# One subtraction per weight stream, moved from VectorE to GpSimd

## The chip, the cores and the metric

The kernel runs on one core of a Trainium2 chip. The metric is the device time of one execution in microseconds, here the median of three runs. The engines are named as in the profile: PE (TensorE), DVE (VectorE), ACT (ScalarE), POOL (GpSimd) and SP (the queue that issues most DMAs).

## The reference, cut to what matters

One decoder layer on 1024 tokens of width 1024. First an input projection feeds retention heads and stick-breaking attention heads, and an output projection follows; then comes a layer of experts (PEER): each token scores 2 x 128 keys in each of 8 heads, keeps 16 experts a head, and sums what these 128 experts give.

```python
proj = h @ w_in                                        # 1024 x 3584
mixed = concatenate([y_ret, y_sb], -1) @ w_out         # 1024 x 1024
x = x + gate1 * mixed
qry = (h2 @ w_query).reshape(T, 8, 2, 128)             # 1024 x 2048
top_s, top_i = top_k(einsum('thpc,hpkc->thpk', qry, sub_keys), 16)
...                                                    # best 16 of the 256 pairs, softmax gates
u = expert_down[ids];  a = einsum('pd,ped->pe', x, u)
v = expert_up[ids];    y = einsum('pe,ped->pd', gelu(a) * gates, v)
```

## The kernel before, in words

The tokens are eight tiles of 128. They go through the layer in three segments: tile 0, tiles 1 to 3, and tiles 4 to 7 (`SEGS`). A segment runs nine streams of projection weights (retention K, Q, V and gate; stick-breaking K, Q, V; two halves of the output projection) and four streams of expert query weights. A stream is 512 columns wide and walks over eight blocks of 128 rows (`kt`, 0 to 7).

In the segments of tiles 1 to 3 and 4 to 7 the matmuls are made in three passes for precision. A weight block `raw` is split into a high part `whi`, which ACT rounds (line 272), and a low part `wlo`, which is `raw - whi` (line 273). Before, the low part of block 0 is made on DVE and those of blocks 1 to 7 on POOL. PE then multiplies high by high, high by low and low by high (lines 277 to 279 or 281 to 283). `whi` and `wlo` have three buffers each, `raw` has two that hold two blocks each. There are 26 such streams, so 208 subtractions, 26 on DVE and 182 on POOL. Tile 0 uses unsplit weights.

The experts are handled in two ways. For tiles 0 to 3 POOL fetches every chosen expert's row by an indirect DMA (line 780, 256 a tile, 1024 in all: 128 of `down`, then 128 of `up`), and DVE multiplies it with the token and sums (line 791, `down`) or adds it, scaled, to the result (line 801, `up`). Each such fetch and its DVE instruction is called a gather here. There are five buffers `g`, so POOL can be at most five gathers ahead of DVE. The other operand of the DVE instruction lies in PSUM. Gathers have no place of their own in the program: they stand at its end, and the scheduler of the framework fills them in among the instructions of the segments and of the dense stage. One edge is written by hand: gathers 480 to 495 may be issued only after a certain POOL instruction of the dense stage (`HOLD`), so the first 480 lie in the segments.

Tiles 4 to 7 go through the dense stage: all 16384 experts are multiplied with the tokens on PE (lines 839 to 841 and 948 to 950). It begins when the last segment has its queries, the 16 best keys of each head (lines 674 to 678, on DVE) and the routing of tile 4 (`topk`).

All instructions of an engine run in the order that the scheduler wrote; an instruction that waits holds up what stands behind it on its engine. The scheduler decides by its own reckoning of durations, so moving one subtraction to another engine also moves its neighbours.

Of the kernel before, what the change touches and what calls it, by code (L numbers as in the profile page):

```python
# [10 lines left out]
F32 = mybir.dt.float32  # L11
# [43 lines left out]
def tile_kernel(ctx, tc, A, out):  # L55
    nc = tc.nc
    ACT, DVE, POOL, PE, SP = nc.scalar, nc.vector, nc.gpsimd, nc.tensor, nc.sync
# [12 lines left out]
    def copy(out_, in_, scale=1.0):  # L70
        ACT.activation(out_, in_, AF.Copy, scale=scale)  # L71

    def pstile(tag, bufs, shape=(128, 512)):
        return ps.tile(list(shape), F32, name=tag, tag=tag, bufs=bufs)
# [155 lines left out]
    def seg_gen(phase, t0, nt, hooks):  # L230
# [5 lines left out]
        def U(shape, dt=F32):  # L236
            return up.tile(shape, dt, name="u", tag="u")
# [10 lines left out]
        def stream(src, c0, lhs, evac, transposed):  # L248

            acc = [pstile("acc", 4) for _ in range(4 if transposed else nt)]  # L250
            for kt in range(KT):
                st, sp = kt == 0, kt == KT - 1
                if whole:
                    if kt % 2 == 0:
                        raw2 = U([128, 2, 512])
                        SP.dma_start(raw2, src[c0 // 512, kt // 2])
                    raw = raw2[:, kt % 2]
                    for i in range(len(acc)):
                        sl = slice(128 * i, 128 * i + 128)
                        if transposed:  # L260
                            PE.matmul(acc[i][:, :n], raw[:, sl], lhs[:, kt], start=st, stop=sp)
                        else:
                            PE.matmul(acc[i], lhs[:, kt, sl], raw, start=st, stop=sp)
                    continue
                if kt % 2 == 0:
                    raw2 = wp.tile([128, 2, 512], F32, name="wraw", bufs=2)
                    SP.dma_start(raw2, src[c0 // 512, kt // 2])
                raw = raw2[:, kt % 2]
                lhs_hi, lhs_lo = lhs
                hi = wp.tile([128, 512], F32R, name="whi", bufs=3)  # L270
                lo = wp.tile([128, 512], F32R, name="wlo", bufs=3)
                copy(hi, raw)
                (POOL if kt else DVE).tensor_sub(lo, raw, hi.bitcast(F32))  # L273
                for i in range(len(acc)):
                    sl = slice(128 * i, 128 * i + 128)
                    if transposed:
                        PE.matmul(acc[i][:, :n], hi[:, sl], lhs_hi[:, kt], start=st, stop=False)
                        PE.matmul(acc[i][:, :n], hi[:, sl], lhs_lo[:, kt], start=False, stop=False)
                        PE.matmul(acc[i][:, :n], lo[:, sl], lhs_hi[:, kt], start=False, stop=sp)
                    else:  # L280
                        PE.matmul(acc[i], lhs_hi[:, kt, sl], hi, start=st, stop=False)
                        PE.matmul(acc[i], lhs_hi[:, kt, sl], lo, start=False, stop=False)  # L282
                        PE.matmul(acc[i], lhs_lo[:, kt, sl], hi, start=False, stop=sp)  # L283
            for i in range(len(acc)):
                evac(i, acc[i])
            if hooks:
                hooks.pop(0)()
# [71 lines left out]
        def ev_rk(i, acc):  # L359
# [3 lines left out]
            POOL.tensor_tensor(hv(rkz[i]), hv(k), zeta[:, :, None].to_broadcast([128, 8, 64]), op=OP.mult)  # L363

        stream(A["w_in"], 512, hT_, ev_rk, False)
        if 0 < t0 < NG:
            mod_pass(5 * D, 2, lambda k: U([128, D]), V)
# [3 lines left out]
        def ev_rq(i, acc):  # L371
            q = V()
            rot(acc, q, t0 + i)
            copy(rqT[i], transpose4(q, ident))

        stream(A["w_in"], 0, hT_, ev_rq, False)
        def ev_rv(i, acc):
            copy(rv[i], acc)

        stream(A["w_in"], 1024, hT_, ev_rv, False)  # L380
        rc = [U([128, 2, 512]) for i in range((nt + 1) // 2)]
        rg = [rc[i // 2][:, i % 2] for i in range(nt)]
# [677 lines left out]
```

## Time and profile before

| | |
|---|---|
| median of 3 runs | 3123.57 us (3121.55 to 3126.93) |
| profiled execution, own time | 3128.33 us |
| its span, first to last instruction | 3126.6 us |
| segment of tile 0 | about 0 to 230 us |
| segment of tiles 1 to 3 | about 230 to 730 us |
| segment of tiles 4 to 7 | about 730 to 1440 us |
| dense stage, with the rest of the gathers | 1440 us to the end |

The profile is one execution with every instruction's start and duration. It is read by stretches: an engine that is busy all of a stretch sets its length; an engine with idle time there waits for something, and the rows say for what.

### The profile page before, as it was taken

To read this page: it belongs to the slowest core of one execution; us is meant where nothing else is said; L and a number is where in the kernel's file an instruction comes from. 1 tells how busy PE (TensorE), PEld (TensorE's weight loads), DVE (VectorE), ACT (ScalarE), POOL (GpSimd) and SP (SyncE) were. 2 spreads that over 40 slices of the span, in tenths; PEclk is the share of its full clock that TensorE was granted. 3 is DMA by queue.
4 is the path that set the end of the run, shared out by engine and by line. 5 is a ranking of instruction groups with operands and counts; after the bars stand their busy time and mean duration, and the time that the engine had idled before them with its cause. 6 is when DMAs were issued, how large, how long until landed. Compare 5 with 4: busy or idle time off the path is not lost. (4 is left out here: it accounts for less than half of the span.)

```text
span 3126.6 us, 38159 instructions
## 1 busy us (share of the span) xinstructions
PE 2688.8 (86%) x12308; PEld 2090.4 (67%) x12308; DVE 2508.4 (80%) x4619; ACT 1289.4 (41%) x2249; POOL 1913.3 (61%) x1590
## 2 busy tenths in 40 slices
PE   6967878788987687796889999899889999999996
PEld 2454654576766345584678877677768788888884
DVE  2269879899988998899899767787886777778778
ACT  1222334344333463433767634343444444444441
POOL 1025876777787766743478656556556666766664
PEclk9978985888987687897989999899999999999998
DMA  8787877998787878851389979798788998899997
GB/s 320 251 309 274 304 241 255 332 359 296 246 279 242 286 219 274 318 213 41 138 314 335 339 287 323 265 326 286 274 319 311 337 353 335 330 346 331 352 334 263
DMA packets 299882, 903.36 MB, mean 289 GB/s; under 512 B 34841, under 2 KB 102425, under 8 KB 279201
## 3 DMA queue, kind: packets, MB, share of 16 engines
q0 software_dynamic: 147456, 536.94, 48.5%
q1 hardware_dynamic: 152224, 363.98, 32.3%
q8 instruction: 97, 1.59, 0.2%
q14 instruction: 105, 0.85, 0.1%
HBM read 848.34 MB, written 52.45 MB: 288 GB/s over the span
## 5 line engine op out<-in xcount | busy, mean ns | idle before, releaser
L780 POOL DMA_INDIRECT g<-in_down_dram,ids x512 | 550.0, 1074 | 420.9 <-DVE g L791 253.7
L780 POOL DMA_INDIRECT g<-in_up_dram,ids x512 | 564.3, 1102 | 396.4 <-DVE gy L801 236.6
L801 DVE SCALAR_TENSOR_TENSOR gy<-g,a,gy 128x1024 f32<-128x1024 f32 x508 | 651.1, 1282 | 92.8 <-DMA g<-in_up_dram,ids 87.5
L791 DVE SCALAR_TENSOR_TENSOR g<-g,gy 128x1024 f32<-128x1024 f32 x512 | 612.8, 1213 | 108.7 <-DMA g<-in_down_dram,ids 107.0
L839 PE MATMUL tp<-Thi,dhi 128*128 128x512 f32 x1024 | 404.5, 395 | 26.3 <-ACT dhi L71 21.7
L948 PE MATMUL acc<-u,p 128*128 128x512 f32 x1024 | 402.7, 402 | 27.7 <-ACT acc L71 16.7
L950 PE MATMUL acc<-u,p 128*128 128x512 f32 x1024 | 389.2, 398 | 30.3 <-DVE p L925 30.3
L949 PE MATMUL acc<-u,p 128*128 128x512 f32 x1024 | 407.1, 400 | 2.9 <-POOL u L826 2.9
L840 PE MATMUL tp<-Tlo,dhi 128*128 128x512 f32 x1024 | 402.6, 393 | 0.0
L841 PE MATMUL tp<-Thi,dlo 128*128 128x512 f32 x1024 | 401.3, 393 | 0.3 <-POOL dlo L826 0.3
L826 POOL TENSOR_TENSOR u<-raw,u 128x1024 fp32r<-128x1024 f32 x128 | 309.3, 2430 | 29.9 <-ACT u L71 28.4
L273 POOL TENSOR_TENSOR wlo<-wraw,whi 128x512 fp32r<-128x512 f32 x182 | 233.9, 1296 | 74.6 <-ACT whi L71 58.4
L826 DVE TENSOR_TENSOR dlo<-raw,dhi 128x1024 fp32r<-128x1024 f32 x122 | 187.6, 1539 | 93.4 <-ACT dhi L71 92.5
L71 ACT ACTIVATE whi<-wraw 128x512 fp32r<-128x512 f32 x208 | 128.6, 629 | 322.3 <-PE acc L283 110.4
L948 PEld LDWEIGHTS acc<-u,p 128*128 128x128 f32 x1024 | 198.6, 194 | 74.8 <-ACT acc L71 19.2
L950 PEld LDWEIGHTS acc<-u,p 128*128 128x128 f32 x1024 | 196.2, 192 | 77.3 <-DVE p L925 36.3
L839 PEld LDWEIGHTS tp<-Thi,dhi 128*128 128x128 f32 x1024 | 194.2, 190 | 68.2 <-ACT dhi L71 23.6
L282 PE MATMUL acc<-wlo,Thi 128*128 128x512 f32 x504 | 213.0, 423 | 26.1 <-POOL wlo L273 24.3
L949 PEld LDWEIGHTS acc<-u,p 128*128 128x128 f32 x1024 | 199.0, 194 | 45.2 <-POOL u L826 3.3
L71 ACT ACTIVATE yacc<-acc 128x512 f32<-128x512 f32 x186 | 109.1, 594 | 283.5 <-PE acc L950 281.7
L841 PEld LDWEIGHTS tp<-Thi,dlo 128*128 128x128 f32 x1024 | 193.6, 189 | 40.9 <-POOL dlo L826 1.4
L840 PEld LDWEIGHTS tp<-Tlo,dhi 128*128 128x128 f32 x1024 | 194.0, 189 | 39.0
(271 smaller groups left out, 5069.8 us busy)
## 6 DMA issues: line engine op xcount, KB each, us to landing
raw<-in_downT_dram SPq DMA_DIRECT2D x64, 1024.0 KB
raw<-in_up_dram SPq DMA_DIRECT2D x64, 1024.0 KB
gd<-u SPq DMA_DIRECT2D x32, 1024.0 KB
gm<-gd SPq DMA_DIRECT2D x512, 64.0 KB
wraw<-in_w_in_dram SPq DMA_DIRECT2D x56, 512.0 KB
u<-in_ada_w_dram SPq DMA_DIRECT2D x46, 512.0 KB
wraw<-in_wq_dram SPq DMA_DIRECT2D x32, 512.0 KB
u<-in_w_in_dram SPq DMA_DIRECT2D x28, 512.0 KB
```

Of the source, the lines that this page charges most:

```text
L71: ACT.activation(out_, in_, AF.Copy, scale=scale)
L273: (POOL if kt else DVE).tensor_sub(lo, raw, hi.bitcast(F32))
L780: POOL.indirect_dma_start(out=g, out_offset=None, in_=A[src], in_offset=bass.IndirectOffsetOnAxis(ap=groups[j // m][0][:, j % m:j % m + 1] ...
L791: DVE.scalar_tensor_tensor(g, g, 1.0, hp, op0=OP.mult, op1=OP.mult, accum_out=a[:, j:j + 1])
L801: DVE.scalar_tensor_tensor(y, g, a[:, j:j + 1], y, op0=OP.mult, op1=OP.add)
L826: eng.tensor_sub(lo, raw, hi.bitcast(F32))
L839: PE.matmul(a, dhi[:, sl], Hhi[:, kt], start=kt == 0, stop=False)
L840: PE.matmul(a, dhi[:, sl], Hlo[:, kt], start=False, stop=False)
L841: PE.matmul(a, dlo[:, sl], Hhi[:, kt], start=False, stop=kt == KT - 1)
L948: PE.matmul(y, phi[:, sl], uhi[:, ds_], start=st and b == 0, stop=False, skip_group_check=True)
L949: PE.matmul(y, phi[:, sl], ulo[:, ds_], start=False, stop=False, skip_group_check=True)
L950: PE.matmul(y, plo[:, sl], uhi[:, ds_], start=False, stop=sp and b == GB - 1, skip_group_check=True)
```

## The change

The low part of block 0 is now made on POOL too, like the other seven. The form of the instruction, its operands and buffers are the same.

```diff
                 copy(hi, raw)
-                (POOL if kt else DVE).tensor_sub(lo, raw, hi.bitcast(F32))
+                POOL.tensor_sub(lo, raw, hi.bitcast(F32))
```

DVE loses 26 instructions and POOL gains 26. The order around them changes too. POOL's order, at the start of the stick-breaking Q stream of tiles 1 to 3 (`wlo_2580` is its block 0, `wlo_2593` its block 1, `s8_2346` a small reciprocal root for the retention heads), before:

```order
L780 DMA g_21419<-in_down_dram,ids_0_4_1422 128x1024
L80 TENSOR_SCALAR s8_2346<-s8_2346 128x8
L81 TENSOR_TENSOR s8_2346<-s8_2346,mhalf_137 128x8
L780 DMA g_21422<-in_down_dram,ids_0_4_1422 128x1024
L273 TENSOR_TENSOR wlo_2593<-wraw_2577,whi_2592 128x512
L780 DMA g_21425<-in_down_dram,ids_0_4_1422 128x1024
```

The same place in the changed kernel:

```order
L780 DMA g_21419<-in_down_dram,ids_0_4_1422 128x1024
L80 TENSOR_SCALAR s8_2346<-s8_2346 128x8
L273 TENSOR_TENSOR wlo_2580<-wraw_2577,whi_2579 128x512
L81 TENSOR_TENSOR s8_2346<-s8_2346,mhalf_137 128x8
L780 DMA g_21422<-in_down_dram,ids_0_4_1422 128x1024
L273 TENSOR_TENSOR wlo_2593<-wraw_2577,whi_2592 128x512
L780 DMA g_21425<-in_down_dram,ids_0_4_1422 128x1024
```

The subtraction of block 0 went in ahead of the second half of the reciprocal root, a gather and the subtraction of block 1; nothing else moved here.

DVE's order near the end of the last segment, as the difference between the two kernels. The rows with `s2` pick the 16 best keys for the last query streams (`v_8319` and following are key scores), `gy` rows are gathers:

```order
-L676 MATCH_REPLACE s2_8339<-tv3_8099,v_8319 128x128
+L801 SCALAR_TENSOR_TENSOR gy_22378<-g_22649,a_21991,gy_22378 128x1024
 L677 MAX tv2_8098<-s2_8333 128x8
 L677 MAX tv3_8099<-s2_8339 128x8
+L801 SCALAR_TENSOR_TENSOR gy_22378<-g_22652,a_21991,gy_22378 128x1024
 L678 MAX_INDEX ix2_8102<-tv2_8098,s2_8333 128x8
 L678 MAX_INDEX ix3_8103<-tv3_8099,s2_8339 128x8
+L801 SCALAR_TENSOR_TENSOR gy_22378<-g_22655,a_21991,gy_22378 128x1024
```

Gathers stand here where none stood. Counted over the order of both kernels, DVE has 468 gathers behind it before, and 460 in the change, when it takes up the scores `v_8319`; both have 480 when the last query stream is through. The lag grows through the stick-breaking attention of tiles 4 to 7: near its beginning it is 311 against 308, at its last cumulative products (line 523) 411 against 403.

DVE's order at the very end of the program, as a difference (`x1f` is the output of the dense tiles, line 807 begins the output of tile 3):

```order
 L958 TENSOR_TENSOR x1f<-x1f,yacc 128x512
-L801 SCALAR_TENSOR_TENSOR gy<-g,a,gy 128x1024 x9
+L801 SCALAR_TENSOR_TENSOR gy<-g,a,gy 128x1024 x10
 L807 TENSOR_TENSOR g<-gy,g 128x1024
 L808 TENSOR_TENSOR g<-g 128x1024
```

One more gather stands behind the last work of the dense stage. In between, in the dense stage, the two orders differ by at most four gathers at any instruction.

## Rows read from the trace of the kernel before

**Rows 1.** The page, busy us of each engine, share of the span, instructions.
```profile
PE 2688.8 (86%) x12308; PEld 2090.4 (67%) x12308; DVE 2508.4 (80%) x4619; ACT 1289.4 (41%) x2249; POOL 1913.3 (61%) x1590
```

**Rows 2.** Busy us by stretch: length, each engine (instructions), granted PE clock, DMA share, GB/s.
```profile
230.00:730.00 500.00, 398.79 (x1764) 295.19 (x1764) 436.78 (x869) 176.53 (x324) 354.08 (x328) 0.83 0.85 296
730.00:910.00 180.00, 150.59 (x657) 119.49 (x657) 179.12 (x424) 73.60 (x113) 129.13 (x118) 0.90 0.78 265
910.00:1330.00 420.00, 319.83 (x1556) 219.18 (x1554) 370.52 (x457) 171.78 (x326) 302.41 (x254) 0.80 0.80 268
1330.00:1440.00 110.00, 81.82 (x403) 68.59 (x401) 109.92 (x638) 33.98 (x58) 36.01 (x31) 0.87 0.40 148
...
2400.00:3050.00 650.00, 646.32 (x2845) 534.67 (x2844) 486.64 (x571) 282.25 (x421) 430.63 (x325) 1.00 0.92 339
```

**Rows 3.** The same stretches, line 273 alone: DVE busy (x count), POOL busy (x count).
```profile
230.00:730.00 500.00, 11.16 (x13) 115.12 (x90) 0.83 0.85 296
730.00:910.00 180.00, 3.35 (x5) 49.75 (x38) 0.90 0.78 265
910.00:1330.00 420.00, 4.90 (x5) 41.01 (x32) 0.80 0.80 268
1330.00:1440.00 110.00, 1.37 (x2) 25.57 (x20) 0.87 0.40 148
```

**Rows 4.** Line 273 by engine: count, ns minimum/median/maximum, first and last start.
```profile
L273 POOL TENSOR_TENSOR wlo<-wraw,whi x182: 1251/1290/1740, 36.8 to 1396.9; 128x512 fp32r<-128x512 f32 x182
...
L273 DVE TENSOR_TENSOR wlo<-wraw,whi x26: 633/693/1825, 36.3 to 1375.4; 128x512 fp32r<-128x512 f32 x26
```

**Rows 5.** Waits from 230 to 1440 us: who <- for whom: us, times, longest.
```profile
POOL g L780 <- DVE g L791: 89.7, 113, 3.3
POOL g L780 <- DVE gy L801: 77.1, 75, 6.4
...
PE acc L282 <- POOL wlo L273: 24.3, 20, 3.5
...
DVE wlo L273 <- ACT whi L71: 13.9, 9, 3.0
...
PE acc L282 <- DVE wlo L273: 1.6, 2, 1.0
```

**Rows 6.** Timelines of DVE, POOL, PE near 380 us: start, us, instruction [idle before].
```profile
379.61 0.71 DVE L273 TENSOR_TENSOR wlo<-wraw,whi 128x512 fp32r<-128x512 f32 x1
...
379.57 1.68 POOL L81 TENSOR_TENSOR s<-s,mhalf 128x8 f32<-128x8 f32 x1
...
382.56 1.28 POOL L273 TENSOR_TENSOR wlo<-wraw,whi 128x512 fp32r<-128x512 f32 x1
...
380.37 0.50 PE L282 MATMUL acc<-wlo,Thi 128*128 128x512 f32 x1 [0.56 <-DVE wlo L273]
...
383.90 0.50 PE L282 MATMUL acc<-wlo,Thi 128*128 128x512 f32 x1 [0.97 <-POOL wlo L273]
```

**Rows 7.** Timeline of PE: first and last of its longer waits for POOL's low parts.
```profile
304.36 0.80 PE L282 MATMUL acc<-wlo,Thi 128*128 128x512 f32 x1 [1.86 <-POOL wlo L273]
...
1274.61 0.50 PE L282 MATMUL acc<-wlo,Thi 128*128 128x512 f32 x1 [1.10 <-POOL wlo L273]
```

**Rows 8.** Timelines of DVE and POOL near 1252 and 1261 us.
```profile
1251.86 1.82 DVE L273 TENSOR_TENSOR wlo<-wraw,whi 128x512 fp32r<-128x512 f32 x1
...
1251.83 1.30 POOL L273 TENSOR_TENSOR wlo<-wraw,whi 128x512 fp32r<-128x512 f32 x1
...
1260.68 1.34 POOL L273 TENSOR_TENSOR wlo<-wraw,whi 128x512 fp32r<-128x512 f32 x1 [2.49 <-ACT whi L71]
```

**Rows 9.** Timelines of ACT and PE where the dense stage begins.
```profile
1438.74 0.26 ACT L746 ACTIVATE ge<-ge 128x64 f32<-128x64 f32 x1 [17.94 <-DVE ge L745]
...
1439.99 0.79 PE L839 MATMUL tp<-Thi,dhi 128*128 128x512 f32 x1 [19.89 <-ACT dhi L71]
```

**Rows 10.** Timeline of DVE at the end: the last gathers.
```profile
3112.47 6.59 DVE L801 SCALAR_TENSOR_TENSOR gy<-g,a,gy 128x1024 f32<-128x1024 f32 x5 [1.11 <-DMA g<-in_up_dram,ids]
```

## The prediction

> **What bounds the kernel now.** I began with the page's busy shares [rows 1]: PE 86%, DVE 80%, POOL 61% of a span of 3126.6 us. No engine is full over the whole span, so the shares settle nothing and the stretches have to be read one by one [rows 2]. From 2400 to 3050 us PE is busy 646 of 650 us at the full clock: there the dense stage is bound by PE, the change has nothing in it, and whatever moves the start of the dense stage moves its end by as much. So the question is when the dense stage begins, and what is left behind it.
>
> It begins at 1440 us. PE's first dense matmul waited 19.9 us for ACT, and ACT had stood for 17.9 us at an exponential that waits for DVE's routing [rows 9]. DVE is busy 109.92 of the last 110 us before that [rows 2]: the beginning is set by DVE. DVE is also full from 730 to 910 us (179 of 180). In the two other stretches it is busy 87% and 88% of the time, and no engine is full: PE 80% and 76%, POOL 71% and 72%. There a loop sets the pace. POOL issues a gather, DVE uses it and frees the buffer, and POOL may issue the next. POOL's largest waits from 230 to 1440 us are those for DVE to free a buffer, 89.7 and 77.1 us in 188 waits [rows 5]. POOL runs the subtractions of line 273 in that same queue, and PE waited 24.3 us, 20 times, for what they produce [rows 5].
>
> **DVE's part.** The change takes 26 subtractions off DVE, median 0.693 us [rows 4], 20.8 us in the four stretches together [rows 3] (25 of them; the last lies at 36 us, far ahead of its use). Where DVE is full, what it no longer does shortens the stretch: 3.35 us (730 to 910) and 1.37 us (1330 to 1440), together 4.7 us. Where DVE has idle time I take nothing: the idle time grows. The bounds of this term are 0 and 20.8 us, and the 13.9 us that DVE stood waiting for ACT ahead of nine of these subtractions [rows 5] could go as well, which makes 34.7 us the outermost gain. I keep 4.7, since the wait for ACT passes to POOL's queue, where the gathers stand behind it.
>
> **POOL's part.** POOL gains 26 x 1.290 = 33.5 us [rows 4]. What matters is who waits behind it. The stick-breaking Q stream of tiles 1 to 3 shows it best [rows 6]. DVE's block 0 starts at 379.61 and ends at 380.32; PE had waited 0.56 us for it. POOL is at that time in an unbroken run that leads to block 1 (382.56 to 383.84), for which PE waits 0.97 us. In the new order block 0 goes in between lines 80 and 81, where POOL starts at about 379.5: it ends at about 380.8, half a microsecond later than now. Line 81, the next gather and block 1 each come 1.29 us later, and PE with them: this stream costs 1.3 us. In the other streams block 0 itself costs nothing, because PE waited for DVE's block 0 only twice in 26 streams, 1.6 us [rows 5]: ACT and DVE had made it while PE was still in the work before. But a POOL that is pushed back at the start may still be behind at blocks 1 to 7. PE's waits for POOL's low parts lie in ten of the 25 streams, the first at 304 us and the last at 1275 us [rows 7]. If POOL never catches up in any of them, ten times 1.29 makes 12.9 us; if it always does, nothing. It has idle time to catch up in, 28 to 29% of these stretches [rows 2], and sometimes inside a stream, as the 2.49 us before the subtraction at 1260.68 [rows 8]; in the stream that I followed there is none. I take half, 6.5 us.
>
> DVE's relief makes buffers free a little earlier, which pulls the gathers' issue forward; that is inside the first term's bounds and I do not count it again.
>
> **The port.** When DVE and POOL subtract at once, one of them stands. At 1251.83 POOL began a subtraction, and DVE's, which began 0.03 us later, took 1.82 us instead of 0.69 [rows 8]: 1.13 us lost. The change takes away one side of such pairs but puts 26 more POOL subtractions beside DVE's other instructions. Most of what stands on DVE there are gathers, which have one operand in PSUM by the program, so I take nothing; the upper end is 1.13 us for each of the seven subtractions in the two full stretches [rows 3], 7.9 us. The Trainium skill (SBUF — State Buffer, "Who interferes with whom") says that a VectorE instruction with two inputs in SBUF contends with a GpSimd instruction that reads SBUF, and that the second to issue waits for the whole instruction. The row at 1251.86 agrees with it; by that rule an estimate for the change would be the upper end, by the operands of the gathers nothing.
>
> **What the scheduler moved.** By the end of the attention of tiles 4 to 7 DVE is eight gathers behind the old order, and it takes them up again in the last stretch, 1330 to 1440 us, where DVE is full. A gather there costs what the last ones cost, 6.59 / 5 = 1.32 us [rows 10]. So eight of them lengthen the last stretch by 10.5 us. The attention, if DVE bounds it, becomes shorter by the same 10.5 us, and the last stretch begins that much earlier. DVE is busy 88% of 910 to 1330 us [rows 2], so this return is likely but not sure. I take zero for the pair, with 10.5 us to either side. At the end of the program one more gather stands behind the dense work. What ends the kernel is that run of gathers on DVE [rows 10]: plus 1.3 us.
>
> **The sum.** -4.7 + 6.5 + 0 + 0 + 1.3 = +3.1 us. The profiled execution took 3128.33 us, 1.7 us more than its span and 4.8 us more than the median of the three runs, so I add the difference to the median: 3123.57 + 3.1, about 3127 us. That is 0.1% above the time before. Faster or slower here means by more than 0.2%, or 6.2 us, about what a measurement of this kernel can tell from no change.
>
> **Rivals.** First, DVE is the bound all the way from 230 to 1440 us, and the waits of the loop are its shadow. For it speak the two largest waits of POOL, both for DVE [rows 5]; against it, that DVE has 63 us idle from 230 to 730 and 50 us from 910 to 1330 [rows 2]. It would give all 20.8 us and lose 1.3 at the end: 3104 us, or about 3113 if half of it comes through. I give it 0.27.
>
> Second, and slower: the eight gathers are not given back. If the attention is paced by POOL's issue or by PE and ACT instead of DVE, it ends as late as before, and the last stretch carries eight gathers more, 10.5 us; with POOL behind in all ten streams the sum is 12.9 + 10.5 + 1.3 - 4.7 = 20.0 us, 3144 us, and with half of the streams about 3137. What decides is the time at which DVE takes up the first scores of the query streams: unless that is 10.5 us earlier than now, the gathers that stand behind it arrive at the start of the dense stage. For it speaks the full DVE right before 1440 us [rows 2, 9]. I give it 0.31.
>
> Third, the port: the new subtractions stop DVE in the full stretches, the 7.9 us above, 3127 + 7.9 = about 3135 us. Against it speaks the operand of the gathers in PSUM; I give it 0.04. That the change does nothing at all would fall within the forecast, since its time is 3124 us.
>
> **How the numbers follow.** The forecast, within 0.2%, has 0.38; faster by over 0.2% 0.27; slower by over 0.2% 0.31 + 0.04 = 0.35. The range goes from 3106 us, near the full gain of the first rival, to 3143 us, near the full loss of the second; beyond these I leave about one in ten on either side. The forecast's own range is 3117 to 3130 us.
>
> **What would show it right or wrong.** Right: line 273 gone from DVE; PE's waits for POOL's low parts up from 24.3 us by 5 to 10 us, in the streams that had them; DVE's share a little lower; the dense stage beginning within about 6 us of 1440. DVE's last full stretch should begin about 10 us earlier and be about 9 us longer. Wrong: a dense stage that begins 15 us or more earlier, with POOL's waits for DVE down, is the first rival; one that begins 10 us or more later after an attention that ends as late as before is the second; DVE subtractions or sums of two SBUF operands that last twice as long beside POOL's would be the third. If the beginning stays and the end moves, the reason lies in the gathers of the dense stage, which I took as unchanged.

## The result, and the profile after

The changed kernel takes 3144.27 us (median of nine runs, 3136.25 to 3159.79) against 3123.57 for the kernel before, a ratio of 1.0078, 95% interval [1.0057, 1.0099]. A second set of runs gave 1.0087 [1.0058, 1.0115]. It is slower by 0.7 to 0.8% (20.7 us between the medians, 24 us by the ratio), and 1.3 us beyond the upper end of the range. The time is that of the second rival, 3144 us. Whether for the rival's reasons is what the experiments had to show.

The profiled execution of the changed kernel is a long one: 3159.4 us. The page's row of busy times (answers [rows 1]), the stretches (answer [rows 2]: length, busy us of PE, its weight loads, DVE, ACT and POOL, granted PE clock, DMA share, GB/s) and line 273 by engine (answers [rows 4]):

```profile
PE 2692.4 (85%) x12308; PEld 2085.1 (66%) x12308; DVE 2500.8 (79%) x4593; ACT 1290.2 (41%) x2249; POOL 1948.7 (62%) x1616
```

```profile
230.00:730.00 500.00, 390.23 (x1744) 286.30 (x1745) 423.02 (x859) 176.62 (x327) 365.52 (x339) 0.83 0.84 293
730.00:910.00 180.00, 147.54 (x648) 118.40 (x647) 177.22 (x419) 71.74 (x112) 136.80 (x122) 0.89 0.80 272
910.00:1330.00 420.00, 328.86 (x1558) 222.22 (x1557) 357.37 (x445) 173.44 (x325) 296.50 (x254) 0.78 0.76 257
1330.00:1440.00 110.00, 89.31 (x430) 74.48 (x428) 104.50 (x512) 34.78 (x59) 51.91 (x47) 0.89 0.57 202
2400.00:3050.00 650.00, 638.91 (x2797) 525.20 (x2797) 493.95 (x575) 282.58 (x423) 426.82 (x323) 1.00 0.92 336
```

```profile
L273 POOL TENSOR_TENSOR wlo<-wraw,whi x208: 1257/1291/2354, 36.2 to 1408.1; 128x512 fp32r<-128x512 f32 x104
```

The 26 subtractions are where they should be, and DVE's share is a point lower. But from 1330 to 1440 us DVE does 512 instructions where it did 638: it is later with the routing. POOL's and PE's waits from 230 to 1440 us (answer [rows 5]; us, times, longest) and the timelines of ACT, PE and DVE where the dense stage begins and where the program ends (answer [rows 9, 10]):

```profile
POOL g L780 <- DVE g L791: 86.4, 96, 4.7
POOL g L780 <- DVE gy L801: 57.8, 66, 5.9
...
PE acc L282 <- POOL wlo L273: 32.8, 23, 3.0
...
PE acc L279 <- POOL wlo L273: 6.9, 5, 2.9
```

```profile
1457.11 0.26 ACT L746 ACTIVATE ge<-ge 128x64 f32<-128x64 f32 x1 [21.76 <-DVE ge L745]
...
1458.36 0.79 PE L839 MATMUL tp<-Thi,dhi 128*128 128x512 f32 x1 [29.25 <-ACT dhi L71]
...
3143.07 6.59 DVE L801 SCALAR_TENSOR_TENSOR gy<-g,a,gy 128x1024 f32<-128x1024 f32 x5 [0.94 <-DMA g<-in_up_dram,ids]
```

The dense stage begins at 1458.36 instead of 1439.99, 18.4 us later, and the end moves by 31. So this profile shows a loss in two places, ahead of the dense stage and inside it, and the second one had no term in my sum but the last gather. How far one profile can show this, e8 tells below.

### The profile page after: what moved, and what is told of

The parts are those of the page before. It is cut to its first block, busy times and chain, and to the rows that moved or that the text cites. A ratio compares the mean times of both kernels' runs of the same rounds, so it can differ in the third digit from the quotient of the medians.

```text
span 3157.7 us, 38151 instructions
## 1 busy us (share of the span) xinstructions
PE 2692.4 (85%) x12308; PEld 2085.1 (66%) x12308; DVE 2500.8 (79%) x4593; ACT 1290.2 (41%) x2249; POOL 1948.7 (62%) x1616
## 4 chain that ended last, share of the span: by engine, by line
DVE 27%; PE 24%; DMA 19%; issue 15%; POOL 11%; ACT 3%; SPq 1%; POOLq 0%; DVEq 0%; ACTq 0%
POOL g L780 7%; DMA g<-in_up_dram,ids 6%; DVE g L791 5%; DVE gy L801 4%; DMA g<-in_down_dram,ids 4%; DMA raw<-in_downT_dram 2%; DMA gm<-gd 2%; PE tp L839 2%; PE tp L840 2%; PE acc L517 2%; PE acc L263 2%; PE tp L841 2%; DVE p L878 2%; DVE dlo L826 2%; PE acc L950 1%
## 5 line engine op out<-in xcount | busy, mean ns | idle before, releaser
L826 POOL TENSOR_TENSOR u<-raw,u 128x1024 fp32r<-128x1024 f32 x128 | 307.0, 2411 | 12.1 <-ACT u L71 10.5
L273 POOL TENSOR_TENSOR wlo<-wraw,whi 128x512 fp32r<-128x512 f32 x208 | 269.4, 1306 | 64.9 <-ACT whi L71 61.2
L826 DVE TENSOR_TENSOR dlo<-raw,dhi 128x1024 fp32r<-128x1024 f32 x122 | 205.0, 1682 | 90.2 <-ACT dhi L71 89.9
L282 PE MATMUL acc<-wlo,Thi 128*128 128x512 f32 x504 | 211.0, 419 | 32.8 <-POOL wlo L273 32.8
```

The costliest lines, as they stand in the source:

```text
L273: POOL.tensor_sub(lo, raw, hi.bitcast(F32))
L826: eng.tensor_sub(lo, raw, hi.bitcast(F32))
```

## The experiments

All ratios are to the kernel before, run beside each on the same chip (its medians there were 3126.6, 3129.4, 3131.0 and 3127.5 us), with 95% intervals. The intervals reach 4 to 9 us to either side, so a smaller difference can't be told. Start of dense stage means PE's first line 839; "+" is the distance to the profile of before.

**First: again, and by parts.** Four kernels: the change unchanged (e1), the change for some streams only (e2, e3), and the change with VectorE doing its subtraction as well (e4).

```diff
e2
-                POOL.tensor_sub(lo, raw, hi.bitcast(F32))
+                (POOL if kt or src is A["w_in"] else DVE).tensor_sub(lo, raw, hi.bitcast(F32))
e3
+                (POOL if kt or src is A["w_out"] else DVE).tensor_sub(lo, raw, hi.bitcast(F32))
e4
+                kt or DVE.tensor_sub(lo, raw, hi.bitcast(F32)); POOL.tensor_sub(lo, raw, hi.bitcast(F32))
```

> The changed kernel once more, unchanged, for a second profile of it. In the first profile the dense stage began 18.4 us later than before and the program ended 31 us later, while the medians of the runs differ by 20.7 us. Theory A (all of the loss arises ahead of the dense stage, and the 12.6 us between 18.4 and 31 are this one execution's own): dense start 1455 to 1462 us, end 18 to 22 us after that of before, ratio 1.005 to 1.008. Rival (the dense stage itself has become longer by some 12 us): the end again moves 10 us or more further than the dense start.

Measured: 3152.11 us, 1.0087 [1.0058, 1.0115]. Dense start 1452.5 (+12.5), end +18.1. The end moved by 5.6 us more than the dense start, between the two expectations; undecided.

> Block 0 is subtracted on GpSimd in the 14 streams of the input projection (rk, rq, rv, rg, K, Q and V of both groups of tiles), and on VectorE as before in the 4 output and 8 query streams. The order of this kernel is level with that of before at the 480th gather: no gather is deferred into VectorE's last full stretch. Theory A (the deferred gathers make the loss, 1.3 us each, with some us of pushed back streams beside them): within 5 us of before, 3121 to 3129, dense start within 5 us of 1440. Theory B (each subtraction in GpSimd's queue costs, 20.7 us / 26 = 0.8 us apiece wherever it stands): 14 subtractions, +11 us, about 3135.

Measured: 3142.03 us, 1.0045 [1.0026, 1.0064], +14 us. Dense start +17.5. Theory A falls in this form: nothing is deferred here, and yet it is slower. Its dense stage has the order of before (the traces agree in order from 1400 us on), so the loss lies ahead of it. What makes it was not tried further.

> Block 0 is subtracted on GpSimd only in the 4 streams of the output projection (o0 and o1 of both groups of tiles), elsewhere on VectorE as before. Only four subtractions move, but the order is four gathers behind that of before at the 480th. Theory A (deferred gathers): 4 x 1.3 = +5 us and one gather more at the end, +1.3: 3129 to 3131, dense start about 1445. Theory B (a price per subtraction, 0.8 us): 4 x 0.8 = +3 us at most, 3124 to 3127.

Measured: 3146.21 us, 1.0067 [1.0039, 1.0096], +21 us, for four subtractions. Theory B falls too: fourteen subtractions cost 14 us, and four cost 21. A price per subtraction can't make that, nor 1.3 us for each of four gathers. What e3 has, like the full change and unlike e2, is a different order of the dense stage: the scheduler's sequence of gathers differs from before's from about the 580th on, and by the traces it is there the same as the changed kernel's.

> The changed kernel with the subtraction of block 0 left on VectorE as well: VectorE writes the tile, then GpSimd writes the same values over it. So GpSimd has the 26 subtractions more, and VectorE is not relieved. Its order is eight gathers behind, as that of the changed kernel. My term for VectorE's relief (4.7 us, only where VectorE is full): 5 us above the changed kernel, 3149. Rival 1 (relief counts over all of 230 to 1440 us): 20.8 us above it, 3165. Rival 2 (relief counts for nothing, GpSimd's queue sets all): level with the changed kernel within 2 us.

Measured: 3156.1 us, 1.0091 [1.0063, 1.0119], 4 us above e1 by the medians and 1 by the ratios. With intervals of 9 us to either side that cannot be told from nothing, nor from the term for VectorE's relief. And it is no clean test: by the traces the scheduler has given e4 an order of its own, which differs from e1's at 2097 of DVE's 4593 places, line 273 left aside. So e4 says nothing on the 20.8 us of the first rival; e5 does.

**Second: the engine and the order apart.** The scheduler makes a new order on all engines as soon as one instruction changes its engine. So I fixed the order: every instruction is told which one it stands behind on its engine, which adds no wait.

```diff
     for t in range(NG):
         gather_tile(t, hold)
+    in_order(tc, ORDER)
...
+def in_order(tc, order):
+    traced, last = list(tc.nc.cur_bb.bb.instructions), {}
+    info = mybir.DependencyInfo(mybir.DependencyClass.NoSync, mybir.DependencyReason.DATA)
+    for n in order:
+        i = traced[n]
+        e = str(i.engine)
+        if e in last:
+            tc.add_manual_dep(i, last[e].name, info, reason="order")
+        last[e] = i
```

`ORDER` is a table of 19,066 instructions. e5 is the changed line 273 with the table of the kernel before, e6 the old line with the table of the changed kernel, e7 the changed line with the new table to about the 480th gather and the old one behind it, and e8 the old line with the old table.

> The subtractions of block 0 on GpSimd, as in the changed kernel, but every engine's instructions in the order of the kernel before (fixed instruction by instruction, with no waits added); each moved subtraction stands in GpSimd's queue where it stood, by the scheduler's sequence, on VectorE. No gather is deferred, nothing else is moved. Theory C (the new order on all engines makes the loss, not the engine that subtracts): my terms for the two engines without the gathers, -4.7 + 6.5, within 6 us of before, 3120 to 3132. Theory B (the 26 subtractions in GpSimd's queue make it, with PE waiting behind them): 15 to 25 us slower, 3140 to 3150.

Measured: 3135.91 us, 1.0031 [1.0008, 1.0055], some 10 us by the ratio. That is between the two theories and in neither window, nearer to C. The 20 us of gain of the first rival are excluded: with 26 subtractions off DVE and nothing else moved, the kernel is slower.

> The other half: the subtractions of block 0 on VectorE, as before, but every engine's instructions in the order of the changed kernel, fixed in the same way; the subtraction stands on VectorE where it stood in the sequence on GpSimd. Theory C (order): 15 to 25 us slower than before, about as the changed kernel, 3140 to 3150, dense start 10 to 18 us late. Theory B (queue of GpSimd): within 6 us of before.

Measured: 3153.74 us, 1.0087 [1.0059, 1.0115]. **The order alone costs as much as the whole change.** VectorE subtracts exactly what it did before, and some 25 us are gone. In the traces its order is the changed kernel's at every place of PE, ACT, DVE and POOL, line 273 left aside.

> The changed kernel, with its own order up to about the 480th gather and the order of the kernel before from there on, on all engines. In the profiles of the changed kernel the end moved by 6 and 13 us more than the dense start. If the order of the dense stage costs that, this kernel is 6 to 13 us faster than the changed kernel: 3134 to 3142. If all the loss lies ahead of the dense stage, it is level with the changed kernel: 3144 to 3150.

Measured: 3143.17 us, 1.0045 [1.0019, 1.0071]. The old order of the dense stage brings back some 12 of the 25 us, between the two expectations.

> The kernel before, with its own order fixed instruction by instruction in the way of the other three: the same program, as a second profile of it and as a control of the comparison. Expected: level with before, within 3 us, dense start 1436 to 1444 us.

Measured: 3130.18 us, 0.9996 [0.9974, 1.0017]: fixing the order costs nothing. But its profile has the dense start at 1448.5, 8.5 us later than the other profile of the same program. That is how far one execution's front moves by itself, so the 12.5 to 18.4 us of single profiles above prove little; the ratios do. The end, too, moved by 5.5 us more than the dense start here, as in e1, with nothing changed.

PE's waits for GpSimd's low parts from 230 to 1440 us in e5 were, in lines 282 and 279:

```profile
PE acc L282 <- POOL wlo L273: 33.4, 27, 3.9
...
PE acc L279 <- POOL wlo L273: 8.1, 5, 2.6
```

and in the second profile of before, e8:

```profile
PE acc L282 <- POOL wlo L273: 26.0, 20, 3.5
...
PE acc L279 <- POOL wlo L273: 7.1, 4, 2.4
```

That is 41.5 against 33.1 us, 8.4 us more, and e5 is slower by 10 us (0.0031 x 3129), within 2.5 to 17. The two agree in size, from one profile of each; e15 below does not repeat it.

**Third: the parts of the order.** The old line 273 in e9 to e11. In e9 and e10 the old table has eight gathers moved, each on POOL and DVE together, between places 388 to 444 (every eighth) and 464 to 478 (every second). e11 has the old table to about the 480th gather and the new one behind it. e12 is e7 with eight gathers moved forward.

> The kernel before, subtractions on VectorE, in its own order on every engine but for one thing: eight gathers (each with its issue on GpSimd and its use on VectorE) are taken out of places 388 to 444 (about 1150 to 1285 us) and stand in the last full stretch of VectorE instead, doubled at places 464 to 478. This is the second rival's mechanism alone. If they are not given back: 8 x 1.32 = +10.5 us, ratio 1.003 to 1.004, and the time from the start of the last query stream to the dense start 7 to 10 us longer. If they are given back (the attention and the output streams end that much earlier): ratio 0.999 to 1.001, with the last query stream starting about 10 us earlier.

Measured: 3143.2 us, 1.0035 [1.0017, 1.0053], +11 us where 10.5 were expected. The other sign, 7 to 10 us more from the last query stream to the dense start, did not come: it was 1.8 us.

> The opposite: the kernel before, with eight gathers taken out of places 464 to 478 in VectorE's last full stretch and put in earlier, doubled at places 388 to 444. If the attention and the output streams have room for them (VectorE is busy 88% there): 10.5 us faster, ratio 0.996 to 0.997, the fastest kernel of the study. If the room isn't there: level, 0.999 to 1.001, with the query streams 10 us later.

Measured: 3140.18 us, 1.0034 [1.0020, 1.0048]. Neither case: it is slower, as much as the opposite move. In its profile the query streams begin 29.6 us later than before (in e8, the program of before, 9.9 us later), and the stretch from there to the dense start is only 3 us shorter. So there was no room: the gathers lengthen the attention and the output streams by more than they save behind them.

That eight gathers cost 11 us in either direction leaves a rival for e9: any disturbance of this order costs that much. What speaks against it is where the time lies. From the first query stream to the dense start it takes 139.3 us before, 5.8 us more in e3 with four gathers deferred, 10.5 to 16.2 us more in all seven profiles of kernels with eight (the changed kernel, e1, e4, e6, e7, e9, e13), and 0.2 to 1.4 us less in the six others with before's order there (e5, e8, e11, e14, e15, e16).

DVE's second gather loop (line 801) in two stretches, 1150 to 1300 and 1300 to 1480 us; length, busy us (gathers), granted PE clock, DMA share, GB/s. First e8, then e9:

```profile
1150.00:1300.00 150.00, 79.78 (x63) 0.87 0.77 262
1300.00:1480.00 180.00, 41.88 (x33) 0.86 0.47 171
```

```profile
1150.00:1300.00 150.00, 71.84 (x56) 0.85 0.74 252
1300.00:1480.00 180.00, 50.00 (x40) 0.84 0.51 181
```

Seven gathers, some 8 us, have gone from the first stretch to the second. PE's first product of the dense stage, e8 and e9:

```profile
1448.50 0.79 PE L839 MATMUL tp<-Thi,dhi 128*128 128x512 f32 x1 [19.89 <-ACT dhi L71]
```

```profile
1462.27 0.80 PE L839 MATMUL tp<-Thi,dhi 128*128 128x512 f32 x1 [19.89 <-ACT dhi L71]
```

In e9 PE's first products of the second of the four query streams come at +6.2 us (in e8 at +8.6) and of the third at +18.6 (in e8 +8.7). It is between these two that the doubled gathers stand. The way of the loss is not quite the changed kernel's. PE's wait ahead of its first dense product is the same 19.89 us in e9 as in e8, and what is new are 8.3 us of waits for POOL's low parts (line 279, four times, after the first query stream has begun); POOL's queue holds the doubled gathers too. In the changed kernel those waits are 0.2 us there, and the wait for the dense stage has grown from 19.89 to 29.25 us (29.2 in e1 and e6 as well).

> The kernel before, subtractions on VectorE, in its own order up to about the 480th gather and in the order of the changed kernel from there on. In the profiles the time from the dense start to the end is 5 to 13 us longer in the four kernels with the changed dense order, and between 3 us shorter and 5 us longer in those with the old one. If the order of the dense stage by itself costs: +6 to +12 us, ratio 1.002 to 1.004, dense start within 10 us of 1440, all of it lost behind that. If it costs only behind the new front (since it comes late): ratio 0.999 to 1.001.

Measured: 3142.99 us, 1.0038 [1.0024, 1.0053], +12 us, with the dense start at 1440.6, 0.6 us from before. All of it lies in the dense stage, since the two orders are the same up to 1824 us of before's trace. PE's waits from 2020 to 2520 us, before:

```profile
PE acc L950 <- DVE p L925: 24.9, 11, 4.4
PE acc L948 <- ACT p L71: 6.3, 3, 3.0
PE acc L948 <- ACT acc L71: 5.0, 3, 2.3
```

and e11:

```profile
PE acc L950 <- DVE p L925: 16.9, 7, 4.7
PE acc L948 <- ACT acc L71: 14.6, 3, 7.7
PE acc L948 <- ACT p L71: 13.2, 6, 4.0
PE acc L950 <- DVE g L791: 4.6, 1, 4.6
PE acc L950 <- issue: 0.8, 1, 0.8
PE acc L949 <- POOL u L826: 0.4, 1, 0.4
```

36.2 us have become 50.5: 14.3 us more, about what the profile lost behind the dense start (13.7). These two profiles lie far apart: the others with the new dense order (the changed kernel, e1, e3, e6, e13) have 42 to 52 us of such waits, and of those with the old one e8 has 39.8, e14 43.9, e16 43.8. Steadier is whom PE waits for: for ACT's copies 19 to 28 us in the six with the new dense order, 7 to 17 in the eleven with the old one. Which of the instructions that were exchanged there does it was not tried.

> As the kernel with the new front and the old dense order (e7, ratio 1.0045), with eight gathers put back from the last full stretch (places 465 to 479) into places 388 to 444, so that its order is no more than about three gathers behind that of before at the 480th. If the deferred gathers are what the new front's order costs: about 7 to 10 us faster than e7, 3133 to 3137, ratio 1.001 to 1.003, as the engine alone. If the new front costs for another reason (GpSimd pushed back, the order of the other engines): as e7, ratio 1.004 to 1.005.

Measured: 3152.47 us, 1.0069 [1.0054, 1.0085]: not faster than e7 but slower. As in e10, gathers put into places 388 to 444 cost more there: the query streams begin 23.5 us after those of before, 18.6 in e7. From there to the dense start it is 8.6 us shorter than in e7, against 10.5 us for eight gathers, so the last stretch did answer to them; the time of the whole did not.

**Fourth: does it add up, and the opposite move.** e13 is the old line 273 with the table of e9 to about the 480th gather and the new table behind it. e14 to e16 have the old table, and

```diff
-                POOL.tensor_sub(lo, raw, hi.bitcast(F32))
+                (DVE if next(BLOCK) in ON_DVE else POOL).tensor_sub(lo, raw, hi.bitcast(F32))
```

where `ON_DVE` holds block 0 of sixteen streams (e14), of the other ten (e15), and of all 26 with sixteen later blocks (e16).

> The two parts of the new order that cost by themselves, put together on the kernel before (subtractions on VectorE): eight gathers deferred into VectorE's last full stretch (e9, ratio 1.0035) and the changed kernel's order from the 480th gather on (e11, 1.0038). Nothing else of the new order is in it. If these two are what the new order costs, the ratio is 1.006 to 1.009, that of the order alone (e6, 1.0087). If the rest of the new front (the order of PE, ScalarE, the queues and VectorE's other work) costs as well: 1.005 or less, with the remainder unexplained.

Measured: 3151.76 us, 1.0085 [1.0055, 1.0115], against 1.0087 for the whole new order. The front is undisturbed in this execution: the second query stream begins 0.3 us after that of before, the third 11.8 us after, the dense stage 17.2 us after. From there to the end this one profile is only 2.0 us longer than before's, so the loss in the dense stage is shown by e11's ratio and not by it.

> The order of the kernel before, fixed; block 0 on GpSimd only in the ten streams in which PE never waited for a low part of GpSimd in the trace of before (rk, rv, V of tiles 1 to 3; rk, rv, K and the four query streams of tiles 4 to 7). Theory queue (GpSimd's 1.29 us counts where PE waits behind it): level, 0.999 to 1.001. Theory per subtraction (0.3 us each, from e5's 8 us / 26, wherever it stands): +3 us, 1.001, not to be told apart by itself, only with the next run.

Measured: 3129.7 us, 1.0010 [0.9993, 1.0026].

> The order of the kernel before, fixed; block 0 on GpSimd only in the other sixteen streams, in which PE did wait for GpSimd. Theory queue: all of what the engine alone cost (e5, 1.0031), 1.002 to 1.004, with PE's waits for GpSimd's low parts 8 us above before. Theory per subtraction: 16/26 of it, 1.002.

Measured: 3131.02 us, 1.0008 [0.9990, 1.0026]. The two are level with each other and with before. PE's waits for GpSimd's low parts rose only here (by lines 282 and 279 38.8 us, in e14 31.0, in e8 33.1), but the time doesn't show it. The expectation by GpSimd's queue (1.002 to 1.004 in e15) is missed. Both together make 1.0018, within the intervals of e5's 1.0031. So the engine's own price is some 10 us by e5 and 6 by the other two, each with 7 to 8 us of uncertainty, and where it arises stays open.

> The opposite of the change, in the order of the kernel before, fixed: sixteen later blocks (1 to 7) for whose low part PE waited, 0.4 to 3.6 us each, 23.8 us together, are subtracted on VectorE instead of GpSimd, besides block 0. VectorE reaches their places in its sequence ahead of GpSimd in the trace of before. If PE's waits for GpSimd are worth what they last: up to 20 us faster, ratio 0.994 to 0.998. If VectorE's 0.69 us each, and its wait for ScalarE's high part ahead of them, take it back: 0.999 to 1.002.

Measured: 3120.55 us, 0.9975 [0.9956, 0.9993], 8 us faster: **the fastest kernel of the study, ahead of both.** The same rows from 230 to 1440 us:

```profile
PE acc L282 <- POOL wlo L273: 9.6, 11, 2.0
...
PE acc L279 <- DVE wlo L273: 6.0, 2, 3.3
...
PE acc L282 <- DVE wlo L273: 5.1, 5, 2.5
...
PE acc L279 <- POOL wlo L273: 3.3, 2, 2.7
```

PE waits 24.0 us for low parts instead of 33.1 in e8 and 31.2 in before (with 1.6 for DVE, [rows 5]), 7 to 9 us less, about the gain. That is a third of the 23.8 us: 11.1 us are now waits for VectorE. That the gain comes from these waits is argued from their size; e15, where they rose by 5.7 us and the time did not, is against too close a reading.

## Why the prediction was wrong

**The scheduler's term, taken as zero, is the step that failed.** I had paired "eight gathers lengthen the last stretch by 10.5 us" with "the attention becomes shorter by the same 10.5 us", and kept 10.5 us to either side. e9 has nothing but this in it and loses 11 us (5 to 17). The price was right in size, though in e9 part of it is paid as PE's waits behind POOL's queue; the return did not come. In the seven profiles with eight gathers deferred the query streams begin between 7.7 us before and 19.2 us after those of before, in the seven with the old order up to there (before itself, e5, e8, e11, e14, e15, e16) between 2.6 us before and 10.5 us after: no return of 10.5 us is to be seen. The reason I gave for it, that DVE is busy 88% there, said too little. A likely one is that DVE's idle time in that stretch is time in which it waits for the loop, and that fewer gathers don't end those waits; no run tests it. In e10, which offers more gathers to the same stretch, the stretch became longer.

**The dense stage, "which I took as unchanged", is the second failed step.** I compared the orders up to the start of the dense stage, where the work moves, and at the very end, and priced one gather (1.3 us). The order in between had changed as well, and by itself costs 12 us (e11). The two together, 1.0035 and 1.0038, make 1.0073; e13 measured 1.0085 with both, the whole new order 1.0087, the changed kernel 1.0078 and 1.0087. Within the intervals nothing else of the order is needed for the changed kernel. That other orders can cost in other ways is shown by e2, whose 14 us neither part explains.

**GpSimd's term.** I took half of ten streams, 6.5 us. The engine alone, in the old order, costs 10 us (2.5 to 17, e5), with 8.4 us more of PE's waits. But e5 holds all that the engines' terms stood for, and these were -4.7 + 6.5 + 0 = 1.8 us, just outside its interval. Together they were too low, by some 8 us; which of them, no run shows. The sign that I named came: PE's waits for POOL's low parts in line 282 rose from 24.3 to 32.8 us. GpSimd's term has an error of count: [rows 5] show line 282 alone, and PE waits for low parts in line 279 too, in the query streams. From 230 to 1440 us of before:

```profile
PE acc L279 <- POOL wlo L273: 5.3, 4, 2.4
```

By line 282 there are twelve streams with such waits, by both lines sixteen, not ten. In the new order this price is not to be seen beside that of the order: the changed kernel (1.0078, 1.0087) and the order alone (1.0087) are level. As far as the intervals tell, the two prices don't add; why not was not tested.

**DVE's term.** 4.7 us of relief. e4 has an order of its own and can't price it, and e5 shows no gain left over. The term is neither confirmed nor refuted; the first rival's forecast, some 20 us faster, is refuted by e5. The sign that I gave for that rival, POOL's waits for DVE going down, came without an earlier dense stage: 166.8 us in before and 162.1 in e8, 144.2 and 134.4 in the changed kernel and e1. The time for half of that gain, about 3113 us, left out the 1.3 us at the end; with them it is 3114.5.

**The port.** The change's loss doesn't need it: e6 has no additional subtraction on GpSimd and is as slow as the change. Nor does e5 show it: up to the dense start DVE is busy 1152.8 us there besides line 273, 1155.1 in e8 and 1159.5 in before. By itself it was not tested.

**The second rival** named the deferred gathers, and that they cost and are not given back is shown. Its 20.0 us were made of 12.9 for pushed back streams, 10.5 for gathers, 1.3 for the last one and 4.7 of relief; the runs put 11 on the gathers and 12 on the dense order. So its time was right by luck, for a reason that is half another one. The deciding point that I named, when the query streams begin, could not be read from one profile: two executions of the program of before differ there by 9.9 us. Steadier is the time from the fourth query stream to the dense start: it is 7.1, 7.2 and 8.3 us longer than before in the profiles of the changed kernel, e1 and e6, and within 0.7 us in e5 and e8. That is where the deferred gathers stand in the changed order, and it would have been the better sign there; in e9 and e13, where they stand further ahead, it is 1.8 us, and only the time from the first query stream on shows them.

## What to carry to other kernels

When a scheduler sets the order, the moved instruction and the new order are two changes; compare the orders over the whole program, and price what has moved in every stage before pricing the instruction. If the order can be fixed, run the instruction alone in the old order and the order alone with the old instruction: these two runs told more here than three variants of the edit (e2 to e4). A long queue with idle time is not a queue with room, and an engine on which another one waits is to be relieved at the places of those waits, not at the places where all cases look alike (block 0).

## What the hardware showed

VectorE can lose several times an instruction's length to GpSimd. The timelines of POOL and DVE in the changed kernel:

```profile
2023.55 4.74 POOL L826 TENSOR_TENSOR u<-raw,u 128x1024 fp32r<-128x1024 f32 x2
```

```profile
2023.98 5.40 DVE L826 TENSOR_TENSOR dlo<-raw,dhi 128x1024 fp32r<-128x1024 f32 x1
```

DVE's subtraction of two SBUF operands (median 1.23 us in before) began 0.43 us after the first of two subtractions on POOL and ended 1.09 us after the second: it stood through both. The Trainium skill (SBUF — State Buffer, "Who interferes with whom") says that the second of two such instructions to issue waits for the whole of the other. The row agrees, and goes further: the waiting instruction was passed by POOL's next one. In the dense stage 20 of 122 of these subtractions took over 2 us in before's profile and 23 in e8's, with the same order, 26 in the changed kernel's and 23 in e1's: which of them meet differs from one execution to the next, and an effect of the order is not to be told from that.

A program's own executions spread by 10 to 36 us here, with the same instructions in the same order. With 9 to 12 runs of a kernel the intervals above still reach 4 to 8 us to either side, and a loss of 8 us can't be placed by one profile.
